# Keeping the adaLN shift out of h: bias columns at evacuation in a hybrid decoder layer on eight cores

## The chip, the cores and the metric

The kernel runs on the 8 NeuronCores of one Trainium2 chip, one sequence of the batch on each core; the cores do not talk to each other. Engine names are those of the profile: PE is TensorE (matmuls), PEld its weight loads, DVE is VectorE, ACT is ScalarE, POOL is GpSimd, SP issues plain DMAs. The metric is device time in microseconds of the slowest core.

A run can fall into a slow state, in which cores of one die or of both get a lower TensorE clock (in the changed kernel's first run, 3368.64 us, cores 4 to 7 have a mean granted clock of 0.903 to 0.907, cores 0 to 3 one of 0.964 or 0.965). Only fast runs are compared. A pair of cores was a little disturbed even in some runs that count as fast, so the stages below are read from **core 2**, which was undisturbed.

## The reference, cut to what matters

```python
cond = silu(c)
mod = cond @ w_mod + b_mod                       # (B, 6D)
sh_a, sc_a, gt_a, sh_m, sc_m, gt_m = split(mod, 6)
h = rmsnorm(x, g_pre_mix) * (1 + sc_a) + sh_a    # the shift sh_a is what the change moves
fq, fk, fv, fg, sq, sk, sv = split(h @ w_in)
fox = forgetting_attention(fq, fk, fv, log_sigmoid(fg + b_forget))     # 8 heads
swa = sliding_window_attention(rope(sq), rope(sk), sv, sinks)          # 8 heads, 2 kv heads
x = x + gt_a * rmsnorm(concat(fox, swa) @ w_out, g_post_mix)
# then a squared-ReLU MLP with its own shift, scale and gate
```

S = D = 2048, head size 128, feed-forward width 8192. Weights lie in DRAM as float32 and are cast to bf16 by the DMA that loads them (the DMA view of the kernel before counts 512 KB for a chunk of 2048 x 128 elements, 2 bytes each).

## The kernel before

The sequence is cut into four tiles of 512 tokens. The kernel has these stages:

1. **Head.** Scale and shift of `mod` are computed in 16 chunks each, as their weights arrive; row m of h for tile 0 is made as soon as its scale and shift are there.
2. **Tiles 1 to 3.** Norm statistics, `z = x*A*rstd`, `h = z + shift`, then q, k and v of head 0 (a head pair for v) and the forget gate.
3. **Heads 0 and 1** of the forgetting attention. The other projections are *fill*: after each attention step some of their matmuls are issued, so that TensorE has work while the exps run.
4. Sliding-window attention, heads 2 to 7, `w_out`, MLP. From `w_out`'s end on TensorE is full.

```python
def n_z(t, k):
    stt(x(k), x(k), Av(0, slice(k, k + 1)), rstd[t % 2](), ALU.mult, ALU.mult)     # VectorE
def n_h(t, k):
    if k % 4 == 3: ts(hT(t, k), x(k), modT(slice(k, k + 1)), ALU.add)              # VectorE
    else:          act(hT(t, k), x(k), AF.Identity, bias=modT(slice(k, k + 1)))    # ScalarE

def next_pj():                       # the projections take turns on two PSUM banks
    b = banks[PJ[pj[0] % 2]]; pj[0] += 1
    return b

def ev_rope(dstf):                   # evacuation of one 512-token tile of a rope stripe
    ...
    act(qrot(p=(0, 64)), bk(p=(64, 128)), AF.Copy)
    act(qrot(p=(64, 128)), bk(p=(0, 64)), AF.Copy)
    tt(bk(), bk(), cosT(sl), ALU.mult)
    tt(qrot(), qrot(), sinT(sl), ALU.mult, eng="pool")
    tt(dstf(sl), bk(), qrot(), ALU.add)

def stripe(i, ev):                   # 128 output columns of w_in: four tiles of 16 matmuls
    s = R1.acq(("A", i))
    for t in range(NT):
        yield from g_fm(s, t, ev(t), t == NT - 1)

F.main = [q_(1), k_(1), stripe(I_SK, ...), vpair(I_SV, vts)] + [four sq stripes]     # fill of head 0
fox(0, 64 * 7 + 128)
F.main = [stripe(I_SK + 1, ...)] + [four sq stripes] + [q_(2), k_(2), vpair(I_V + 2, vY)]
fox(1, 64 * 7 + 128)
```

Each attention step is: scores on TensorE into one of two score banks, a subtract on VectorE (the decay row), an exp on ScalarE, then two matmuls.

## Time and profile before

The kernel takes 3196.54 us (median of three fast runs, 3195.72 to 3197.28). These are two rows of the page of the kernel before, on its slowest core; each row has 40 slices of 80 us and a digit is the busy share of a slice in tenths (PEclk: the granted TensorE clock in tenths).

```profile
PE   1467989998888898999999999999999999999993
...
PEclk9678999999999998999999999999999999999997
```

TensorE has slack in the first 4 slices and some in slices 5 to 17; then it is full until the last slice. The next lines are the windows view of core 2, cut at the stages (two of them left out): busy time of each engine in each stretch, then the granted clock, the share of the DMA engines, and GB/s.

```profile
core 2: us, PE busy (x) PEld busy (x) DVE busy (x) ACT busy (x) POOL busy (x), PEclk, DMA share, GB/s
0.00:120.00 120.00, 36.85 (x487) 21.21 (x493) 16.06 (x56) 18.03 (x18) 19.91 (x41) 0.94 1.00 187
120.00:213.00 93.00, 45.47 (x295) 22.87 (x299) 36.53 (x66) 39.54 (x46) 0.53 (x1) 0.67 0.45 124
...
277.50:621.40 343.90, 317.79 (x1797) 163.95 (x1830) 121.77 (x194) 109.64 (x184) 77.67 (x90) 0.98 0.48 83
```

| stretch (core 2) | us | what it is |
|---|---|---|
| 0 to 277.5 | 277.5 | head, tiles 1 to 3, up to head 0's first exp |
| 277.5 to 621.4 | 343.9 | heads 0 and 1 with their fill |
| 621.4 to 3188.0 | 2566.6 | everything after |

In the head the DMA engines are the limit (share 1.00), and TensorE does 37 us of work in 120. No clock should be read from the head: the trace holds clock records only from about 92 us on, and where it holds none the column counts full speed. The last chunk of the head, a shift chunk, is used at 158 us (the last scale chunk just before it, at 157), as this line of the timeline of TensorE on the slowest core shows (start, duration, what, and in brackets the idle time before it and what ended it):

```profile
158.37 0.57 PE L385 MATMUL bank<-condpad,rmod_84 128*128 128x1 bf16 x16 [0.60 <-DMA rmod_84<-wMA]
```

Head 0 then waits for the forget-gate row, which goes through DRAM. In the timeline of core 2 its next scores wait 10.31 us for the first exp; in the chain of waits of the slowest core the wait before that exp is the load of the row:

```profile
278.28 0.37 PE L385 MATMUL bank<-qT_72,kT_73 128*128 128x256 bf16 x1 [10.31 <-ACT Pb_93 L402]
...
267.89 15.17 DMA cfb_80<-crow
```

The chain of waits through one rope tile, on core 2 (start, us, what):

```profile
380.62 0.59 ACT qrot L402
381.22 0.60 ACT qrot L402
381.96 1.27 POOL qrot L405
383.45 0.55 issue
384.00 0.70 DVE bank L405
384.82 0.66 issue
385.48 0.59 ACT qrot L402
```

Copies, sine product, subtract ("DVE bank L405" at 384.00), a piece marked "issue" in which the exp of the attention step falls, and 4.86 us after the first copy the next tile's first copy. This ring turns once per rope tile; over the stage the commonest distance between the first copies of two tiles is 4.87 us.

### The profile page before, as it was taken

To read this page: it belongs to the slowest core of one execution; us is meant where nothing else is said; L and a number is where in the kernel's file an instruction comes from. 1 tells how busy PE (TensorE), PEld (TensorE's weight loads), DVE (VectorE), ACT (ScalarE), POOL (GpSimd) and SP (SyncE) were. 2 spreads that over 40 slices of the span, in tenths; PEclk is the share of its full clock that TensorE was granted. 3 is DMA by queue.
4 is the path that set the end of the run, shared out by engine and by line. 5 is a ranking of instruction groups with operands and counts; after the bars stand their busy time and mean duration, and the time that the engine had idled before them with its cause. 6 is when DMAs were issued, how large, how long until landed. Compare 5 with 4: busy or idle time off the path is not lost.

```text
span 3194.3 us, 37768 instructions; the slowest of 8 cores (3185.7 to 3194.3 us)
## 1 busy us (share of the span) xinstructions
PE 2866.9 (90%) x14323; PEld 1367.1 (43%) x14592; DVE 886.2 (28%) x1403; ACT 769.4 (24%) x1244; POOL 519.2 (16%) x650
## 2 busy tenths in 40 slices
PE   1467989998888898999999999999999999999993
PEld 1224533666433343444444444444444444444441
DVE  1142344344444455643111100000133211000005
ACT  1152234264445434533111100000111111000000
POOL 1000233000000155530000011111100000111113
PEclk9678999999999998999999999999999999999997
DMA  9924545633334833364445455555688644545456
GB/s 187 205 67 90 91 75 83 93 53 52 68 65 76 139 106 119 141 130 73 76 76 78 75 99 94 98 95 97 133 190 191 113 77 75 78 74 79 74 97 199
DMA packets 99203, 325.76 MB, mean 102 GB/s; under 512 B 12080, under 2 KB 12208, under 8 KB 92624
## 3 DMA queue, kind: packets, MB, share of 16 engines
q0 software_dynamic: 58320, 211.87, 43.1%
q1 hardware_dynamic: 40704, 111.46, 10.8%
q8 instruction: 118, 1.93, 0.2%
q14 instruction: 61, 0.50, 0.1%
HBM read 493.12 MB, written 42.01 MB: 168 GB/s over the span
## 4 chain that ended last, share of the span: by engine, by line
PE 79%; DVE 5%; DMA 5%; issue 4%; ACT 4%; POOL 2%; SPq 0%; DVEq 0%; POOLq 0%; ACTq 0%
PE bank L385 79%; DMA rmod_84<-wMA 3%; DVE bank L405 1%; POOL qrot L405 1%; ACT qrot L402 1%; DMA bfg<-b_fg 1%; POOL acc_194 L405 1%; DVE bank L410 1%; ACT rr L402 1%; DVE mixF L410 1%; DVE xstB L410 1%; ACT sqA L402 0%; DMA cfb_80<-crow 0%; DVE mix L405 0%; ACT Pb_97 L402 0%
## 5 line engine op out<-in xcount | busy, mean ns | idle before, releaser
L416 DVE TENSOR_SCALAR bank<-bank 128x512 f32<-128x512 f32 x256 | 166.1, 695 | 645.9 <-PE bank L385 623.7
L419 DVE COPY mixF<-bank 128x512 f32<-128x512 f32 x64 | 41.2, 686 | 842.8 <-PE bank L385 790.1
L402 ACT ACTIVATE sq_191<-bank 128x512 f32<-128x512 f32 x59 | 35.2, 597 | 827.1 <-DVE mixF L419 793.0
L385 PE MATMUL bank<-mix,rung_117 128*128 128x512 bf16 x1002 | 225.7, 380 | 1.1
L385 PE MATMUL bank<-mix,rung_116 128*128 128x512 bf16 x1004 | 225.2, 379 | 1.1
L385 PE MATMUL bank<-mix,rung_119 128*128 128x512 bf16 x1004 | 225.0, 379 | 1.1
L385 PE MATMUL bank<-mix,rung_118 128*128 128x512 bf16 x1004 | 224.9, 379 | 1.1
L405 DVE TENSOR_TENSOR bank<-bank,cfb_82 128x512 f32<-128x512 f32 x192 | 119.4, 630 | 127.2 <-PE bank L385 121.1
L385 PEld LDWEIGHTS bank<-mix,rung_117 128*128 128x128 bf16 x1024 | 100.2, 98 | 123.1 <-issue 3.1
L385 PEld LDWEIGHTS bank<-mix,rung_118 128*128 128x128 bf16 x1024 | 100.4, 98 | 121.0 <-issue 0.6
L385 PEld LDWEIGHTS bank<-mix,rung_119 128*128 128x128 bf16 x1024 | 100.4, 98 | 120.7
L385 PEld LDWEIGHTS bank<-mix,rung_116 128*128 128x128 bf16 x1024 | 100.2, 98 | 120.8
L385 PE MATMUL bank<-hT,ring_69 128*128 128x512 bf16 x566 | 142.2, 381 | 3.5 <-DVE mix L405 2.6
L385 PE MATMUL bank<-hT,ring_67 128*128 128x512 bf16 x433 | 117.1, 404 | 10.1 <-DVE mix L405 6.2
L405 DVE TENSOR_TENSOR bank<-bank,cfb_80 128x512 f32<-128x512 f32 (+3 forms) x128 | 74.0, 596 | 83.0 <-PE bank L385 70.6
L405 POOL TENSOR_TENSOR acc_193<-acc_193,sq_191 128x512 f32<-128x512 f32 x59 | 74.7, 1266 | 122.5 <-ACT sq_191 L402 122.5
L385 PE MATMUL bank<-qT_72,kT_73 128*128 128x512 bf16 (+3 forms) x151 | 52.7, 349 | 34.0 <-ACT Pb_93 L402 21.8
L385 PE MATMUL bank<-hT,ring_71 128*128 128x512 bf16 x312 | 78.4, 385 | 4.9 <-DVE mix L405 4.0
L405 POOL TENSOR_TENSOR acc_194<-acc_194,sq_192 128x512 f32<-128x512 f32 x59 | 74.5, 1262 | 46.6 <-ACT sq_192 L402 44.8
L385 PEld LDWEIGHTS bank<-hT,ring_69 128*128 128x128 bf16 x576 | 54.9, 98 | 63.3 <-issue 7.3
L385 PE MATMUL bank<-qT_89,kT_90 128*128 128x512 bf16 (+3 forms) x154 | 55.0, 359 | 21.2 <-ACT Pb_93 L402 7.5
L385 PEld LDWEIGHTS bank<-hT,ring_67 128*128 128x128 bf16 x448 | 44.1, 102 | 67.3 <-issue 29.2
(660 smaller groups left out, 4685.6 us busy)
## 6 DMA issues: line engine op xcount, KB each, us to landing
rung_116<-wU POOLq DMA_DIRECT2D x32, 512.0 KB, 5.8
rung_117<-wU POOLq DMA_DIRECT2D x32, 512.0 KB, 5.8
rung_118<-wU POOLq DMA_DIRECT2D x32, 512.0 KB, 5.8
rung_119<-wU POOLq DMA_DIRECT2D x32, 512.0 KB, 5.7
rung_116<-wD POOLq DMA_DIRECT2D x32, 512.0 KB, 5.7
rung_117<-wD POOLq DMA_DIRECT2D x32, 512.0 KB, 5.6
rung_118<-wD POOLq DMA_DIRECT2D x32, 512.0 KB, 5.6
rung_119<-wD POOLq DMA_DIRECT2D x32, 512.0 KB, 6.1
```

The source lines that it names most:

```text
L385: ins = e.matmul(o, lhsT=l, rhs=rh, start=st, stop=sp)
L402: return P.op("act", lambda e: e.activation(out=out.ap, in_=in_.ap, func=func, **kw), r, [out])
L405: return P.op(eng, lambda e: e.tensor_tensor(out=out.ap, in0=a.ap, in1=b.ap, op=op), [a, b], [out])
L410: return P.op("dve", lambda e: e.scalar_tensor_tensor(out=out.ap, in0=a.ap, scalar=sc, in1=b.ap, op0=op0, op1=op1), r, [out])
L416: return P.op(eng, lambda e: e.tensor_scalar(out=out.ap, in0=a.ap, scalar1=sc, scalar2=None, op0=op), r, [out])
L419: return P.op("dve", lambda e: e.tensor_copy(out=out.ap, in_=a.ap), [a], [out])
```

## The change

The intent: the shift need not be in h. `h @ W = z @ W + W^T shift`, and `W^T shift` is one column per stripe. So the 16 shift chunks need not arrive before h can be made; they load behind x. The column is added when a projection leaves PSUM. In the forgetting attention it goes into the bias of the evacuation for q, is dropped for k (it changes a row of scores by a constant), goes into the bias of the exp for heads 0 and 1, whose q is evacuated too early, and for v goes through attention unchanged and ends as a bias of `w_out`. In the sliding-window attention it is added in the two rope products for q and k, and at evacuation for v. What follows the forget gate's matmuls leaves the tile loop, the statistics get two buffers, and q, k of head 1 and a v pair move ahead of head 0, because the shift must be known before the gate can be finished.

The core of the diff (cut):

```diff
+    def n_sq(t, q):
+        act(sqA[q % 2](), xs_of(t)(slice(4 * q, 4 * q + 4)), AF.Square)
 ...
     def n_z(t, k):
-        x = xs_of(t)
-        stt(x(k), x(k), Av(0, slice(k, k + 1)), rstd[t % 2](), ALU.mult, ALU.mult)
-
-    def n_h(t, k):
-        ...
+        stt(hT(t, k), xs_of(t)(k), Av(0, slice(k, k + 1)), rstd[t % 2](), ALU.mult, ALU.mult)
 ...
+    def col(out, slot_bufs, lhs):
+        bk = next_pj()
+        pe([mm(bk(0, 1), lhs(k), shb(slice(k, k + 1)), k == 0, k == KC - 1) for k in range(KC)], slot_bufs + [shb()], [bk()])
+        return bk
 ...
+    def sw_bias(i, b):
+        bk = fm_col(b)
+        act(bs(slice(i, i + 1)), bk(0, 1), AF.Copy)
+        act(bsw(slice(i, i + 1), p=(0, 64)), bk(0, 1, p=(64, 128)), AF.Copy)
+        act(bsw(slice(i, i + 1), p=(64, 128)), bk(0, 1, p=(0, 64)), AF.Copy)
 ...
-                tt(bk(), bk(), cosT(sl), ALU.mult)
-                tt(qrot(), qrot(), sinT(sl), ALU.mult, eng="pool")
+                stt(bk(), bk(), bs(slice(i, i + 1)), cosT(sl), ALU.add, ALU.mult)
+                stt(qrot(), qrot(), bsw(slice(i, i + 1)), sinT(sl), ALU.add, ALU.mult)
 ...
-    def stripe(i, ev):
+    def stripe(i, ev, bias=None):
         s = R1.acq(("A", i))
+        if bias:
+            bias(R1.bufs[s])
 ...
+            for q in range(4):                                   # tile loop: work on tile t + 1
+                at(5 + 3 * q, lambda q=q: n_sq(t + 1, q))
+                at(8 + 3 * q, lambda q=q: n_stat(t + 1, q))
+            at(18, lambda: n_rstd(t + 1))
+            for k in range(KC):
+                at(19, lambda k=k: n_z(t + 1, k))
 ...
-    F.every = 8
+    F.every = 6
-    F.main = [q_(1), k_(1), stripe(I_SK, sk_ev(0)), vpair(I_SV, vts)] + [stripe(I_SQ + i, sq_ev(i)) for i in range(4)]
-    fox(0, 64 * 7 + 128)
+    F.main = [sk_(0), svpair(), sq_(0), sq_(1), sq_(2), sq_(3)]
+    fox(0, 64 * 5 + 128)
```

## The prediction

> **What bounds the kernel now.** From 1,410 us on, TensorE is 99.5% busy (windows view); the change leaves that alone. The slack is earlier:
>
> - Head, 0 to 164 us: TensorE works about 50 us; the DMA engines are busy throughout (share 0.96, windows). The 32 chunks of scale and shift weights arrive 3.0 to 3.6 us apart, 5.9 while x tile 1 loads too; the last is used at 158.4 us (timeline).
> - Tiles 1 to 3, 164 to 285 us: 34 to 35 us each for about 17 us of projections; four serialized statistics steps, z and h (about 0.7 us a row each) hold TensorE. Then 15 us of waiting for the forget-gate row from DRAM (chain of waits).
> - Heads 0 and 1, 285 to 627 us: 1,152 fill matmuls x 0.2155 = 248 us, attention some 50, modulation 16: 314 of 342 us. Rope evacuation sets the pace, a tile per 4.87 us in the chain.
>
> **What the change does.**
>
> 1. The shift chunks leave the head. 22 half-megabyte loads plus x must arrive before the last scale chunk, not 37. At the read rate seen (330 to 350 GB/s of float32) it lands at about 109 us; tile 0 ends at about 113 instead of 164.
> 2. h is written by one VectorE operation, statistics are double-buffered, the forget gate leaves the loop: tiles of 27 us; the 17-us gap before tile 1 becomes 3. z stays serial (16 x 0.67 us), so 8 us a tile still show. Tile 3 ends at about 196.
> 3. q1, k1 and v (256 units, 55 us) move ahead of head 0, with 16 shift slots (0.43 us each, timeline near 303 us). Head 0 starts at about 267, not 285; the gate wait is hidden.
> 4. Heads 0 and 1 carry 896 units: minus 55 us. Against that, ten rope stripes begin with a bias column of 16 matmuls: 0.41 us as chunk pairs show, 26 ns each[...]. Dearer: the column uses up one turn of two PSUM banks, so the next tile waits for the previous rope chain, about 3 us x 9. The sine product moves from POOL (1.27 us) to VectorE (0.7). Net: 286 to 303 instead of 342.
> 5. Later: q columns, v columns (two pairs loaded again), 128 one-column matmuls for w_out's bias: plus about 11 us.
>
> Sum: 18 earlier at head 0, 47 saved in heads 0 and 1, 11 lost later: **minus 54 us, 3143 us**, 8 in 10 within 3115 to 3170. Chances: faster by over 2% 0.33; within 2% 0.65; slower 0.02.
>
> **Clock.** [...] Before, the granted clock is 0.50 to 0.67 between 120 and 200 us; I expect above 0.8 from tile 1 on. If wave 0 stays at half clock, add 8 us.
>
> **What would show it.** Last scale matmul at 104 to 115 us; tile 3 ends at 190 to 205; head 0's first exp at 260 to 275 without a DMA wait; sliding-window attention starts at 550 to 575 instead of 625; TensorE waits for rope results at stripe starts; after 1,410 only a constant shift.
>
> **What would make it wrong.** Rope on VectorE, which also subtracts for the exps, could lengthen the rope period beyond 4.9 us (plus 20); the stall at stripe starts could be absent (minus 25) or appear at q stripes too (plus 10); shift weights could arrive late before head 0 (plus 10 to 20); x loads could delay the scale chunks further (plus 10).

Marked cuts are passages that no trace of this case shows. None is a term of the sum, which stands whole: 18 earlier, 47 saved, 11 lost, minus 54 us.

## More of the kernel before

The start of head 0 varies by core in this kernel, from 276.5 us on core 1 and 277.5 on core 2 to 284.0 on core 4 (median 282.2); the length of the stage of heads 0 and 1 does not (343.0 to 344.5 us on the eight cores).

In heads 0 and 1 TensorE is busy 318 of 344 us. What it waits for there is the rope evacuation, as the largest line of that kind in the waits view shows (total us, times, longest):

```profile
PE bank L385 <- DVE mix L405: 12.7, 21, 1.5
```

## The result

The changed kernel is not faster. Its first four runs were 3368.64, 3295.49, 3213.46 and 3212.61 us, of which the first two are slow; two more fast ones were 3211.61 and 3211.49. The ratio of its fast runs to the fast runs of before is 1.0049, with a 95% interval of 1.003 to 1.0069: within 2% of before, and slightly slower. (A ratio here is the mean time of one kernel's fast runs over that of the other's in the same rounds, so it is not quite the ratio of the quoted medians.) The prediction was 3143 us.

Its first profile fell in the slow state. This is a stretch of the MLP, where TensorE is full, on core 4 of that run (windows view, columns as before):

```profile
2300.00:2900.00 600.00, 600.00 (x2387) 253.25 (x2385) 125.86 (x192) 76.42 (x128) 44.66 (x79) 0.85 0.53 103
```

The granted clock, the third number from the right, is 0.85; in the 800 us before it was 1.00. Since such a stretch tells nothing about the change, the kernel was run again (e1_after below, ratio 1.0062, 1.0039 to 1.0085), and all that follows is from its fast profile. There core 2 has 1,500 us of full TensorE at 1.00, 6,948 matmuls of 216 ns (the same view):

```profile
1500.00:3000.00 1500.00, 1500.00 (x6948) 679.99 (x6947) 223.00 (x342) 169.12 (x284) 175.26 (x265) 1.00 0.54 99
```

First the same rows of the page as shown of before, slowest core:

```profile
PE   1798887998888898999999999999999999999994
...
PEclk9889988999999998899999999999999999999997
```

Then two stretches in the windows view of core 2, columns as before:

```profile
120.00:213.00 93.00, 75.75 (x390) 36.52 (x391) 38.43 (x58) 18.98 (x15) 5.40 (x11) 0.82 0.41 88
...
286.80:627.70 340.90, 290.05 (x1645) 138.95 (x1646) 142.43 (x224) 112.30 (x210) 25.35 (x48) 0.91 0.48 82
```

| stage, core 2 | before | after | change | predicted change |
|---|---|---|---|---|
| up to head 0's first exp | 277.5 | 286.8 | +9.3 | -18 |
| heads 0 and 1 | 343.9 | 340.9 | -3.0 | -47 |
| everything after | 2566.6 | 2580.2 | +13.6 | +11 |
| sum | 3188.0 | 3207.9 | +19.9 | -54 |

By the median of the eight cores the four changes are +4.2, -1.4, +14.4 and +18.5: core 2 started head 0 early in the profile of before (in e3 and e8 below, which have the same head, it starts at 283.6 and 284.1). The length of the stage of heads 0 and 1 agrees within 4 us on all undisturbed cores of every fast profile.

The head did shrink: the timeline of TensorE of the changed kernel, core 2, has the last scale chunk, now the last chunk of the head, at 114 us; before, the last chunk came at 158. The long wait before it is for a chunk whose load queues behind six loads of stripes (four of them for tile 0) and shares the DMA engines with x of the next tile:

```profile
90.25 0.57 PE L387 MATMUL bank<-condpad,rmod 128*128 128x1 bf16 x16 [36.15 <-DMA rmod<-wMA]
...
114.06 0.55 PE L387 MATMUL bank<-condpad,rmod 128*128 128x1 bf16 x16
```

But tiles 1 to 3 take 31.0, 33.1 and 29.5 us. This is a part of the chain of waits there, core 2 (the same columns as above):

```profile
150.50 10.69 DVE hT L412 x16
...
161.33 21.56 PE bank L387 x116
...
183.59 10.69 DVE hT L412 x16
```

All 16 z rows of the next tile stand in a row, 10.69 us on VectorE, and most of the tile's TensorE work, 21.6 us for tile 2, comes after them. Tile 3 ends at 212 us. Then come q1, k1, the v pair and the shift chunks, and head 0 starts no earlier than before, only with 55 us more of the matmuls done (256 x 0.2155 us, the prediction's figure).

Heads 0 and 1 therefore had 256 of 1,152 fill matmuls less to do, and took the same time. TensorE's work in the stage fell from 318 to 290 us, its clock from 0.98 to 0.91. The waits in the stage, core 2:

```profile
PE bank L387 <- DVE mix L407: 26.1, 6, 4.5
PE bank L387 <- DVE skT L407: 8.6, 2, 5.0
...
PE bank L387 <- DVE bq L418: 4.8, 1, 4.8
```

The first two are the waits for rope: eight, up to 5 us long, where they were at most 1.5. The third is the same kind of wait at the column of head 2's q. One of the eight in the timeline of core 2:

```profile
370.79 1.03 PE L387 MATMUL bank<-hT,ring 128*128 128x512 bf16 x4
...
371.69 0.54 PE L387 MATMUL bank<-shb,ring 128*128 128x1 bf16 x16
...
375.76 0.69 DVE L407 TENSOR_TENSOR mix<-bank,qrot 128x512 bf16<-128x512 f32 x1
...
376.59 1.86 PE L387 MATMUL bank<-hT,ring 128*128 128x512 bf16 x4 [4.37 <-DVE mix L407]
```

At 371.69 the bias column of the next rope stripe takes its turn of one projection bank. The first tile of that stripe needs the other bank, which the previous tile's rope still holds; its sum ends at 376.45, and TensorE idles 4.37 us. The four matmuls after it take 1.86 us, where the four at 370.79 took 1.03; the clock records say one half from 375.2 to 382.0 us.

### The profile page after: what moved, and what is told of

It is laid out like the page before. It is cut to its first block, busy times and chain, and to the rows that moved or that the text cites. A ratio compares the mean times of both kernels' runs of the same rounds, so it can differ in the third digit from the quotient of the medians.

```text
span 3293.9 us, 38871 instructions; the slowest of 8 cores (3234.5 to 3293.9 us)
## 1 busy us (share of the span) xinstructions
PE 3004.6 (91%) x15016; PEld 1403.2 (43%) x15016; DVE 915.4 (28%) x1452; ACT 749.9 (23%) x1229; POOL 469.0 (14%) x614
## 4 chain that ended last, share of the span: by engine, by line
PE 82%; DVE 6%; ACT 3%; issue 3%; DMA 3%; POOL 2%; SPq 0%; DVEq 0%; ACTq 0%; POOLq 0%; another core or an unknown queue 0%
PE bank L387 82%; POOL acc_209 L407 2%; DMA rmod_83<-wMA 2%; DVE bank L407 1%; DVE hT L412 1%; ACT qrot L404 1%; DMA xstA<-xP 1%; DVE bank L412 1%; DVE mixF L412 1%; ACT rr L404 1%; DVE qrot L412 1%; DMA rsh_89<-wMB 0%; ACT sq_206 L404 0%; DMA cfb_82<-crow 0%; ACT Pb_98 L404 0%
## 5 line engine op out<-in xcount | busy, mean ns | idle before, releaser
L387 PE MATMUL bank<-mix,rung_128 128*128 128x512 bf16 x1024 | 247.4, 404 | 0.0
L387 PE MATMUL bank<-mix,rung_127 128*128 128x512 bf16 x1024 | 245.3, 402 | 0.0
L387 PE MATMUL bank<-mix,rung_129 128*128 128x512 bf16 x1024 | 244.6, 401 | 0.0
L387 PE MATMUL bank<-mix,rung_130 128*128 128x512 bf16 x1024 | 243.8, 400 | 0.0
L404 ACT ACTIVATE sq_206<-bank 128x512 f32<-128x512 f32 x30 | 17.9, 597 | 797.8 <-DVE mixF L421 797.8
L387 PEld LDWEIGHTS bank<-mix,rung_128 128*128 128x128 bf16 x1024 | 105.3, 103 | 138.1 <-issue 67.9
L387 PE MATMUL bank<-hT,ring_69 128*128 128x512 bf16 x512 | 141.1, 409 | 23.3 <-DVE mix L407 13.1
L387 PEld LDWEIGHTS bank<-mix,rung_127 128*128 128x128 bf16 x1024 | 104.7, 102 | 135.3 <-issue 62.1
L387 PEld LDWEIGHTS bank<-mix,rung_129 128*128 128x128 bf16 x1024 | 104.3, 102 | 135.4 <-issue 61.0
L387 PEld LDWEIGHTS bank<-mix,rung_130 128*128 128x128 bf16 x1024 | 104.2, 102 | 134.1 <-issue 56.8
L387 PE MATMUL bank<-hT,ring_68 128*128 128x512 bf16 x384 | 100.3, 393 | 4.8 <-DVE mix L407 4.4
L387 PE MATMUL bank<-hT,ring_71 128*128 128x512 bf16 x320 | 86.1, 400 | 8.6 <-DVE mix L407 8.6
L387 PEld LDWEIGHTS bank<-hT,ring_69 128*128 128x128 bf16 x512 | 51.5, 104 | 82.7 <-issue 38.9
L407 DVE TENSOR_TENSOR mix<-bank,rr 128x512 bf16<-128x512 f32 x48 | 33.2, 692 | 89.3 <-ACT rr L404 89.3
```

Of the source, the lines that this page charges most:

```text
L387: ins = e.matmul(o, lhsT=l, rhs=rh, start=st, stop=sp)
L404: return P.op("act", lambda e: e.activation(out=out.ap, in_=in_.ap, func=func, **kw), r, [out])
L407: return P.op(eng, lambda e: e.tensor_tensor(out=out.ap, in0=a.ap, in1=b.ap, op=op), [a, b], [out])
```

## The experiments

Ten runs, in three calls (e1 to e4, e5 to e8, e9 and e10), each on another chip; kernels of one call shared the runs of the kernel before, whose fast runs lie between 3194.6 and 3198.2 us in all three but for one with disturbed cores. Stages are from core 2. The ratio is of whole runs, slightly disturbed fast ones too (e2 and e3 above all), so the stages are the cleaner reading.

| run | what | stage of heads 0, 1 (us) | core 2 in all (us) | ratio to before, 95% interval |
|---|---|---|---|---|
| before | | 343.9 | 3188.0 | |
| e1_after | the change | 340.9 | 3207.9 | 1.0062, 1.0039 to 1.0085 |
| e2_nocol | no columns in rope stripes (wrong result) | 308.7 | 3175.1 | 0.9967, 0.991 to 1.0024 |
| e3_beforecol | before, with columns | 380.7 | 3228.3 | 1.0194, 1.0161 to 1.0227 |
| e4_sbcol | columns in the score banks | 304.2 | 3175.2 | 0.9972, 0.994 to 1.0005 |
| e5_sinpool | e4, sine product on POOL | 311.0 | 3180.0 | 0.9954, 0.9907 to 1.0001 |
| e6_poolrope | e4, rope sum on POOL, bank freed early | 276.3 | 3144.2 | 0.9852, 0.9799 to 0.9906 |
| e7_earlyz | e6, z spread over the tile | 279.3 | 3132.6 | 0.9777, 0.9707 to 0.9847 |
| e8_beforepool | before, rope as in e6 | 320.4 | 3169.3 | 0.9918, 0.9864 to 0.9973 |
| e9_final | e7 again | 277.2 | 3125.3 | 0.9805, 0.9787 to 0.9822 |
| e10_nolate | e9 without the later columns (wrong result) | 278.7 | 3108.7 | 0.9747, 0.9732 to 0.9763 |

### e1_after: the change again

No edit. It is the control and gave the fast profile shown above.

> The changed kernel once more, for a profile in the fast state and as the control of the other runs. Theory A (stall): a rope stripe now begins with its bias column; the column takes one of the two turns of the projection banks, so the next tile waits for the whole rope evacuation of the tile before (4.4 us each)[...]. That eats the 55 us of matmuls that were moved out of heads 0 and 1. Theory B (rope on VectorE): the sine product now on VectorE lengthens each rope tile and so sets the pace. Theory C (exp latency): heads 0 and 1 are bound by the attention chain, whatever fill they carry. All three expect 3211 us here, with head 0's first matmul at about 286 us and sliding-window attention at about 627 us, also in the fast state.

Measured: fast runs of 3213.36, 3214.57 and 3221.18 us; head 0's first exp at 286.8 us and sliding-window attention at 627.7 us.

### e2_nocol: the rope stripes without their column

```diff
+    P.op("dve", lambda e: e.memset(bs().ap, 0.0), [], [bs()])
+    P.op("dve", lambda e: e.memset(bsw().ap, 0.0), [], [bsw()])
     def sq_(i):
-        return stripe(I_SQ + i, ev_rope(...), lambda b: sw_bias(i, b))
+        return stripe(I_SQ + i, ev_rope(...))
     # the same for sk_
```

> Changed kernel without the bias columns of the ten rope stripes (their biases are zero, so the result is wrong on purpose); everything else stays, sine product on VectorE too. A: heads 0 and 1 shorten from 342 to about 290 us and the kernel to 3155 to 3170 us, the waits of TensorE for rope results at stripe starts vanish, the granted clock of the stage returns to about 0.98. B or C: about 3205 us, since only 10 x 0.5 us of matmuls go.

Measured: the stage takes 308.7 us instead of 340.9 and core 2 is 32.8 us faster. The result is wrong, as intended. The stage in the windows view, core 2:

```profile
286.40:595.10 308.70, 276.00 (x1485) 130.05 (x1485) 141.63 (x224) 107.47 (x180) 25.36 (x48) 0.95 0.52 90
```

The columns cost 32.2 us, of which their matmuls are about 4 (10 times 0.41, an estimate from the chunk pairs before). By the two windows lines 18.2 us are idle time of TensorE (50.9 against 32.7) and 14.0 busy time: the columns' 4, the rest with the lower clock. Theories B and C, which gave the columns 5 us, fall as the whole cause. But A's 290 us was too low by 19: something else holds the stage as well, and the clock is 0.95, not 0.98. (The column of head 2's q was left in; TensorE waits 5.0 us there.)

### e3_beforecol: the kernel before, with a column

```diff
     def stripe(i, ev, column=False):
         s = R1.acq(("A", i))
+        if column:                       # True for the ten rope stripes
+            bk = next_pj()
+            pe([mm(bk(0, 1), b(...), c.re(condpad.h[:, k, 0:1]), k == 0, k == KC - 1) for k in range(KC)], [b(), c], [bk()])
+            act(dmy(...), bk(0, 1), AF.Copy)        # three small copies, as in the change
```

> The kernel before, with a bias column of 16 one-column matmuls (and its three small copies) put at the start of each rope stripe, result unused, so the output stays right. A: 10 stalls of 3 to 4.4 us[...], 3225 to 3250 us. B or C: 3200 to 3205 us, 5 us of added matmuls and copies.

Measured: the stage 380.7 us, 36.8 more than before, and the result is right. The line of the waits view that answers to the one of before, core 2:

```profile
PE bank L385 <- DVE mix L405: 29.8, 13, 4.9
```

These waits grow from 12.7 to 29.8 us in total, the longest from 1.5 to 4.9, and the clock drops from 0.98 to 0.94. The stall belongs to the column's turn of the bank and not to anything else in the change: it appears alone in the kernel before.

### e4_sbcol: the columns in the score banks

```diff
+    turn = [next_pj]
+    def score_turn():
+        b = banks[SB[St.sb % 2]]
+        St.sb += 1
+        return b
     def col(out, slot_bufs, lhs):
-        bk = next_pj()
+        bk = turn[0]()
 ...
+    turn[0] = score_turn                 # from head 0 on; also for the sliding-window v column
```

> Changed kernel, right result: the columns that fall into the attention stages take a turn of the two score banks instead of the two projection banks; the same matmuls, copies and order otherwise. A: nearly all of what the run without columns gains, 3160 to 3180 us; a short wait for an exp may show in place of the wait for rope. B or C: 3205 to 3215 us.

Measured: right, stage 304.2 us, core 2 at 3175.2 us. The same matmuls in another bank save 36.7 us in the stage, a little more than e2, for head 2's q column moved too. So not the column but its place cost the time. The stage in the windows view, and one rope tile in the chain of waits, core 2:

```profile
287.00:591.20 304.20, 276.78 (x1645) 133.54 (x1646) 141.79 (x224) 111.87 (x210) 25.36 (x48) 0.96 0.54 92
```

```profile
407.89 0.59 ACT qrot L404
...
409.19 0.76 DVE bank L412
409.94 0.66 DVE qrot L412
...
411.31 0.70 DVE bank L407
...
412.80 0.59 ACT qrot L404
```

TensorE has 277 us of work here and the stage takes 304. The chain shows the ring of before again: copies, cosine product, sine product, the sum, the subtract at 411.31, the exp in the gap after it, and 4.91 us after 407.89 the next copies at 412.80. The sine product has moved from POOL into VectorE, and the ring is as long as it was.

### e5_sinpool: the sine product back on POOL

```diff
-                act(qrot(p=(0, 64)), bk(p=(64, 128)), AF.Copy)
+                act(qrot(p=(0, 64)), bk(p=(64, 128)), AF.Identity, bias=bs(slice(i, i + 1), p=(64, 128)))
                 # the other half likewise
-                stt(qrot(), qrot(), bsw(slice(i, i + 1)), sinT(sl), ALU.add, ALU.mult)
+                tt(qrot(), qrot(), sinT(sl), ALU.mult, eng="pool")
```

Here ScalarE adds the bias in the copy.

> The run with columns in the score banks (3175 us on its undisturbed cores, heads 0 and 1 in 304 us), with the sine product given back to POOL and its bias added by ScalarE in the copy. Right result if ScalarE reads the bias by the partitions of its input; if not, wrong result but the same timing. Theory B (the move of the sine product to VectorE costs time): heads 0 and 1 shorten by 10 us or more. Theory D (ring of waits: subtract on VectorE, exp and two copies on ScalarE, rope on VectorE, then the next subtract, 4.9 us a tile whichever engine takes the sine): within 6 us of 304, since POOL's 1.27 us replaces VectorE's 0.66 in the same ring.

Measured: right, stage 311.0 us, 6.8 more than e4 (5.8 by the median of the cores). The bias was given at the partitions of the copy's input (64 to 127 for an output at 0 to 63); the other way was not tried. Two first copies that follow each other in the chain of waits, core 2:

```profile
409.07 0.68 ACT qrot L404
...
414.14 0.69 ACT qrot L404
```

Theory B falls here: with the sine product back on POOL the stage is no shorter. My limit for D was 6 us, and core 2 is just beyond it. The edit changed two things, though: each copy, now with a bias, takes 0.68 us where it took 0.59, twice per tile. That is about 7 us over 40 tiles (an estimate) and the whole of the ring's growth from 4.91 to 5.07 us, so the engine of the sine product by itself is worth about nothing.

### e6_poolrope: a shorter ring

```diff
+                r, c = (qrot, accs[0])[rp[0] % 2], sqb[rp[0] % 2]      # two buffers each
-                stt(bk(), bk(), bs(slice(i, i + 1)), cosT(sl), ALU.add, ALU.mult)
-                stt(qrot(), qrot(), bsw(slice(i, i + 1)), sinT(sl), ALU.add, ALU.mult)
-                tt(dstf(sl), bk(), qrot(), ALU.add)
+                stt(c(), bk(), bs(slice(i, i + 1)), cosT(sl), ALU.add, ALU.mult)
+                tt(r(), r(), sinT(sl), ALU.mult, eng="pool")
+                tt(dstf(sl), c(), r(), ALU.add, eng="pool")
```

> As the run before in this list, but the cosine product goes to a buffer in SBUF (two of them, and two for the sine), so that the bank is free after one VectorE operation, and the sine product and the last sum are both on POOL; the VectorE queue has one rope operation a tile instead of three and never waits for POOL. D: the ring is shorter (about 3.4 us a tile), TensorE sets the pace with 268 us of work: heads 0 and 1 in 270 to 282 us, kernel 3143 to 3155 us. If exp latency bounds the stage (theory C): unchanged at 304.

Measured: right, stage 276.3 us, core 2 at 3144.2 us, both as D expected:

```profile
286.60:562.90 276.30, 267.54 (x1645) 133.72 (x1646) 89.42 (x144) 120.22 (x210) 127.17 (x128) 0.98 0.63 102
```

TensorE is busy 267.5 of 276.3 us. POOL does far more than before (127 us), but nothing on VectorE waits for it any more. The ring was worth 27.9 us on core 2 (25.6 by the median of the cores). Theory C, that exp latency bounds the stage, falls. The edit does three things at once (an earlier free bank, two operations a tile fewer on VectorE, two buffers each); which of them matters was not taken apart.

### e7_earlyz and e9_final: z spread over the tile

```diff
             for q in range(4):
-                at(5 + 3 * q, lambda q=q: n_sq(t + 1, q))
-                at(8 + 3 * q, lambda q=q: n_stat(t + 1, q))
-            at(18, lambda: n_rstd(t + 1))
+                at(2 + q, lambda q=q: n_sq(t + 1, q))
+                at(4 + q, lambda q=q: n_stat(t + 1, q))
+            at(8, lambda: n_rstd(t + 1))
             for k in range(KC):
-                at(19, lambda k=k: n_z(t + 1, k))
+                at(9 + k * 11 // 16, lambda k=k: n_z(t + 1, k))
```

> As the run before in this list, and the statistics of the next x tile come at the start of a tile and its z is spread over the second half, instead of all 16 z at the end. If the serial z (10.7 us in the chain at the end of tiles 1 and 2) is what made tiles 31 to 33 us long instead of my 27: tile 3 ends 15 to 20 us earlier, head 0 starts at 265 to 272 us, kernel 12 to 20 us faster than the run before. If TensorE or the shift loads bind there instead: less than 5 us.

> The kernel of the run e7_earlyz unchanged, right result: columns in the score banks, rope products in SBUF with the sum on POOL, statistics and z spread over the tile. Its profile fell in the slow state and it had only two fast runs (3129.8 and 3128.9 us); this is for a fast profile and an interval: 3125 to 3135 us, head 0 at about 268 us and sliding-window attention at about 548 us on all cores.

e7 had two fast runs (3129.81 and 3128.88 us) and a slow profile. e9, the same kernel, has a fast one: fast runs of 3131.13 to 3139.02 us, ratio 0.9805. All its cores ended between 3123.7 and 3129.4 us in the profile. Head 0's first exp on core 2 comes at 266.7 us, 19.9 earlier than in e6 (18.5 by the median of the cores), and sliding-window attention at 543.9. Tile 3 ends at 191 us instead of 212. The tile stretch in the windows view, core 2:

```profile
120.00:213.00 93.00, 86.35 (x493) 43.68 (x494) 38.21 (x58) 20.27 (x19) 8.57 (x17) 0.94 0.66 127
```

In the chain of waits the z rows made during tile 1 now come in pieces of 1 to 5 rows, at most 2.9 us each, where they were 10.69 us in one piece. In the tile stretch TensorE does 86 us of work, where e1 did 76, at clock 0.94 instead of 0.82.

### e8_beforepool: the shorter ring in the kernel before

The rope edit of e6 without the biases, in the kernel before.

> The kernel before with only the rope evacuation of the run e6 (products to SBUF, sum on POOL). D: the ring binds in the kernel before as well, heads 0 and 1 shorten from 342 to about 320 us (TensorE work is 316), kernel about 3170 us. If it doesn't bind there: 3195 us. It also tells how much of a faster version is owed to the change and how much to the rope.

Measured: right, stage 320.4 us instead of 343.9 (windows view, core 2):

```profile
284.10:604.50 320.40, 315.57 (x1829) 165.39 (x1830) 96.36 (x154) 110.35 (x184) 128.46 (x130) 0.98 0.52 88
```

The ring held the kernel before too, for 23.5 us. With the ring out of both, the stage is 44 us shorter with the change (320.4 to 276.3; 41 by the medians of the cores); with the ring in both and no columns (before against e2) only 35.

### e10_nolate: without the later columns

```diff
     def q_(h):
-        return stripe(I_Q + h, ev_q(h), lambda b: q_bias(h, b))
+        return stripe(I_Q + h, ev_q(h))                    # biases set to zero once
-    F.main = [vpair(I_V + 6, vX, True)]                    # and the other pair, and vbias(0), vbias(1)
+    F.main = [vpair(I_V + 6, vX)]
-            if t == 0:                                     # w_out's bias: 16 x 8 one-column matmuls
+            if False:
```

> The kernel of the run e9_final without the bias columns that come after heads 0 and 1: q columns of heads 2 to 7, v columns of all pairs but the shared one (with the two stripe pairs that are loaded again for it), and the 128 one-column matmuls for the bias of w_out; those biases are zero, so the result is wrong on purpose. I predicted 11 us for them; the stretch after heads 0 and 1 is 16 to 18 us longer than before on undisturbed cores. If the columns are all of it: 14 to 19 us faster than e9_final. If the modulation slots that now come every 6 instead of every 8 fills, or the order, are part of it: 11 us or less.

Measured: wrong as intended; the median of the fast runs is 3116.5 us against 3132.8, 16.3 us. The stretch after heads 0 and 1 goes from 2581.4 to 2564.4 us by the median of the cores, 17 us (19.6 on core 2). The columns, with the stripes loaded again for them, are all of the later loss, which I had priced at 11.

## Why the prediction was wrong, point by point

- **The head (step 1): right.** The last scale chunk was predicted to land at about 109 us and to be used at 104 to 115; it was used at 114.
- **"tiles of 27 us ... Tile 3 ends at about 196" (step 2): wrong in size.** I saw that z stays serial, and counted 8 us of it beside a tile too short. The chain of tile 2 has 10.69 us of z and then 21.6 us of TensorE work, 32 in sum. Tile 3 ended at 212. e9 shows it from the other side: with z spread, head 0 starts 18 to 20 us earlier, at 266.7, where the prediction had it (267). The gate wait was indeed hidden.
- **"Net: 286 to 303 instead of 342" (step 4): this step failed most.** Its terms were minus 55 us of fill, plus 27 for stalls and 4 for column matmuls. That makes 318, not 286 to 303; for the other 15 to 32 us the only term it names is the sine product leaving POOL, and for that it gives no sum (0.57 us on 40 tiles would be 23). The runs give: fill out and sine moved, minus 35.2 (before to e2), where 70 to 87 were credited; columns, plus 32.2 (e2 to e1), where 31 was charged. So the charge for the columns was right, and so was its mechanism, a turn of two banks; that the sums agree so closely is in part luck. There were eight stalls of 3.6 to 5.0 us where I said 9 of 3, but they replaced shorter waits of the ring, so idle time grew by 18 us only; of the other 14, about 10 go with the lower clock (0.91 against 0.95 in e2), which I had not charged.
- **The credits of the same step: wrong, and this made most of the miss.** The sine move is worth about nothing: the ring took 4.87 us before and 4.91 after. And 55 us of matmuls bring 35, because the ring of rope and attention, not TensorE, paces much of the stage. Of the 20 us that did not come, 6.6 are more idle time of TensorE (26.1 us before, 32.7 in e2), about 3 new matmuls of the change, and most of the rest goes with the clock, 0.98 to 0.95 (estimates from the windows lines and the matmuls counted in the traces). I had written "rope evacuation sets the pace" two paragraphs earlier and then subtracted TensorE time as if it did not. e6 and e8 show the ring at 28 and 23.5 us.
- **Later (step 5): plus 11 predicted, 13.6 measured in the change, 17 by taking the columns out of e9.** Mis-sized, in the right direction.
- **Clock: right where it was stated** (0.82 from tile 1 to 213 us against 0.67 before), and missed where it mattered: the stage of heads 0 and 1 fell to 0.91. In the trace the four matmuls right after the 4.37-us wait took 1.86 us, where four before it took 1.03, and e3 lowers the clock of the kernel before from 0.98 to 0.94. The clock in the records is 1 or one half here: 61 us of the stage are at half clock, against 24 in e4, in pieces of 3.4 or 6.8 us; part of that time TensorE was idle anyway. What sets the clock was not shown: in the tile loop of e1_after the records say one half from 122.6 to 132.9 us on core 2, where TensorE, following the z rows, never waits longer than 2.1 us (timeline):

```profile
120.83 1.02 PE L387 MATMUL bank<-hT,qh 128*128 128x512 bf16 x4 [2.00 <-DVE hT L412]
123.97 1.86 PE L387 MATMUL bank<-hT,qh 128*128 128x512 bf16 x4 [2.12 <-DVE hT L412]
126.62 1.87 PE L387 MATMUL bank<-hT,qh 128*128 128x512 bf16 x4 [0.79 <-DVE hT L412]
```

The account of the miss of 74 us on core 2 (minus 54 predicted, plus 19.9 measured): about 27 lie in the start of head 0, of which 18 to 20 are the z rows by e9 and some 5 to 7 that core 2 started head 0 earlier than most cores before; 44 lie in heads 0 and 1; 3 later.

Left open: what the 16 late shift chunks cost by themselves was not isolated. Nor was the earlier z tried in the kernel before, so how much of the best version's 1.95% is owed to the change cannot be said exactly: the rope edit alone gives the kernel before 0.8% (e8).

e9_final is right, and faster than both kernels; whether by 2% over the kernel before is not clear (its interval, 0.9787 to 0.9822, holds 0.98).

## What to carry to other kernels

A small operation that takes a turn of a double buffer can cost a wait for the holder of the other buffer, here 4.4 us for 0.41 us of matmuls; give it a place whose holder is quick, as the 36.7 us between e1 and e4 show for unchanged work. Before subtracting an engine's removed work from a stage, ask which ring of waits turns there: if another engine's ring sets the period, part of the removed work comes back as idle time and as a lower clock, here some 17 of 55 us. A row of operations at the end of a tile that the next tile waits for is exposed, here for 18 to 20 us over two tiles; spread it over the tile before.
